# A ninth slot of weights, one late weight instead of two: a Hymba layer (RG-LRU beside window attention) on one Trainium2 core

## The chip, the cores and the metric

The kernel runs on one core of a Trainium2 chip. The metric is device time in microseconds (us) of one execution; the time of a version is the median of its runs. PE is the matrix engine, DVE the vector engine, ACT the activation engine, POOL the general engine, SP the engine that issues the transfers; PEclk is the clock that PE was granted, as a share of 2.4 GHz (its other level is 1.2 GHz).

## The reference, cut to what matters

One layer on a prompt of 4096 positions (width 1024) and 8 sample positions, in fp32:

```python
xn = rms_norm(x, g_pre)
proj = xn @ w_in     # rnn 512 | rnn gate 512 | q 512 | k 128 | v 128 | attention gate 512
# recurrent group: width-4 causal conv, then
#   h_t = a_t*h_{t-1} + sqrt(1-a_t^2)*(i_t*x_t),  a_t = sigmoid(L)^(8 r_t)
# attention group: window of 128, 8 q heads, 2 kv heads, bucketed bias, a sink per head
y = x + rms_norm(concat(h * silu(gate_r), o * silu(gate_a)) @ w_out, g_post)
```

The sample positions attend to a cache of 128 rows, and the states and windows are outputs too.

## The kernel before, in words

Every fp32 operand of a product is split into a high and a low part, and `mm3` (L122, L123, L124) makes one product of three matmuls. The prompt is cut into 11 chunks (ten of 384 columns, and the first of 256 with the 8 sample columns). Three stages follow each other.

**The recurrent stage** goes over the chunks. `load_A` loads row tiles `xs` (L153; four slots), ACT squares them (L161, `sq`), POOL scales them, `prep_A` transposes them on PE (L176, `pt`) into `xh`/`xl`, which are also stored for the second stage. `proj_A` makes the products `pr` with eight weights, four for the recurrent input and four for its gate; ACT copies a product out (`xr` L298, `xc` L302). `rnn_A` makes the gates (`gt`), with ACT's `thr`, `thi` (L333, L334). `scan_A` takes one square root over four tiles (L348, `uu`, ahead of which ACT loads another function table), scans (L352), multiplies (L361) and stores `hh` to `mix_d` (L362).

**The attention stage** goes over the chunks again: keys `pk`, values `pv`, four queries `pq` and four gates `pga` from ten weights, then for each block of 128 the scores `S` (L601, L602), a softmax (`tt`), its transpose `pT` (L635) and the output `po` (L644). For chunk 0 the order is V, Q0, K, Q1, Q2, Q3, G0, G1, G2, G3, and weight numbers run V=13, Q=8 to 11, K=12, G=14 to 17. **The output stage** (L819 to L821) multiplies by `w_out`, whose tiles of `mix_d` come through staging tiles `xf`.

A weight is loaded by `load_w`: a transfer of 512 KB into one of two staging slots `ws` (L105), a copy on ACT (`wh`, L111) and a subtraction on DVE (`wl`, L112). `wh` and `wl` are slots of the pool `wpool`. It has eight, which the recurrent stage's eight weights fill; a weight of the attention stage gets one when the last product with an old weight is done. Eight of the ten weights fit. The last two, G2 and G3, lie in the pool `pbl`, which is opened over the recurrent stage's late buffers (`uu`, `xc`, `sg`, `thr`, `thi`, `tt`, `aa`, `hh`), so these two can only be written when that stage's last buffers are free.

The order of the instructions isn't written by hand. A scheduler puts each engine's list in an order of its own, by a model of the machine, and each engine then runs its list strictly in that order. A change of the pools therefore changes the lists of all five engines. Names in the lists carry chunk and column tile: `gt_10_2` is the gate of chunk 10, tile 2; a number behind that tells buffers apart.

Of the kernel before, what the change touches and what calls it, by code (L numbers as in the profile page):

```python
# [9 lines left out]
F32 = mybir.dt.float32  # L10
# [5 lines left out]
P = 128  # L16
D = 1024
KD = D // P
DR = 512
HD = 64  # L20
NH = 8
# [3 lines left out]
NSAMP = 8  # L25
SEQ = 4096
STEP = 384
# [17 lines left out]
def hymba_kernel(ctx: ExitStack, tc: tile.TileContext, ins, outs):  # L45
# [15 lines left out]
    act = nc.scalar.activation  # L61

    const = ctx.enter_context(tc.tile_pool(name="const", bufs=1))
    wpool = ctx.enter_context(tc.tile_pool(name="wpool", bufs=8))
    xpool = ctx.enter_context(tc.tile_pool(name="xpool", bufs=12))
    stage = ctx.enter_context(tc.tile_pool(name="stage", bufs=2))
    dram = ctx.enter_context(tc.tile_pool(name="dram", bufs=1, space=bass.MemoryType.DRAM))
# [15 lines left out]
    def ps_t(n):  # L83
        if phase[0] == "A":
            return ps[2].tile([P, 512], F32, tag="t", name=n, bufs=2)
        return ps[1].tile([P, 512], F32, tag="t", name=n, bufs=1)

    def ps_v(n):
        if phase[0] == "A":
            return ps_t(n)  # L90
        return ps[1].tile([P, 512], F32, tag="v", name=n, bufs=1)
# [11 lines left out]
    def load_w(src, n, pool, bufs=None, spare=None, eng=nc.vector, fast=False):  # L103
        ws = (spare or stage).tile([P, KD, P], F32, tag="ws", name=f"ws_{n}")
        nc.sync.dma_start(ws, src)  # L105
        wh = pool.tile([P, KD, P], F32R, tag="wh", name=f"wh_{n}", bufs=bufs)
        wl = pool.tile([P, KD, P], F32R, tag="wl", name=f"wl_{n}", bufs=bufs)
        if fast:
            nc.vector.tensor_copy(wh, ws)
        else:  # L110
            act(wh, ws, AF.Copy)  # L111
        eng.tensor_sub(wl, ws, wh)  # L112
        return wh, wl

    def load_w_in(m, pool=None, bufs=None, spare=None, eng=nc.vector, fast=False):
        return load_w(w_in_v[:, :, m * P:(m + 1) * P], f"in{m}", pool or wpool, bufs, spare, eng, fast)
# [101 lines left out]
        return p1, p2  # L218


    grow = stage.tile([KD, P], F32, tag="xf", name="grow", bufs=4)
    nc.sync.dma_start(grow, norm_pre.rearrange("o (k p) -> (o k) p", p=P))
    cp0 = ps_t("cp0")
    nc.tensor.transpose(cp0[:, 0:KD], grow, ident[:KD, :KD])
# [5 lines left out]
    xA = ([], [])  # L230
    prep_A(0, xn, range(KD), xA)

    crow = stage.tile([32, P], F32, tag="xf", name="crow", bufs=4)
    nc.sync.dma_start(crow[0:16, :], conv_w.rearrange("o t (c p) -> (o t c) p", p=P))
    nc.sync.dma_start(crow[16:20, :], conv_b.rearrange("o (c p) -> (o c) p", p=P))
    nc.sync.dma_start(crow[20:24, :], b_ga.rearrange("o (c p) -> (o c) p", p=P))
# [133 lines left out]
    ksT = const.tile([P, NSAMP], F32, name="ksT")  # L370
    vsT = const.tile([P, NSAMP], F32, name="vsT")
# [44 lines left out]
    wB = {}  # L416
# [24 lines left out]
    for ci in range(NCH):  # L441
        for item in A_ORDER:
            f, s = item[0], st[ci]
            c = int(item[1:] or 0)
# [55 lines left out]
    def prep_B(ci, src, on_act, half=()):  # L500
        t0, npt, ns = chunks[ci]
        W = npt + ns
        xh, xl = [], []
        for k in range(KD):
            xf = stage.tile([P, STEP], F32, tag="xf", name=f"xf_{src.name}_{k}", bufs=4)
            nc.sync.dma_start(xf[:, :W], src[:, k, :])
            h, l = split_x(xf[:, :W], W, f"{src.name}_{k}", on_act, k in half)
            xh.append(h)
            xl.append(l)
        return xh, xl  # L510
# [169 lines left out]
        return {"K": key, "V": value, "Q": query, "G": gate, "U": unit, "M": scale}  # L680

    def attend_sample(pool):
        def window(new, cache, dst, n):
            pr = ps_t(f"pr_{n}")
            nc.tensor.transpose(pr[:NSAMP, 0:P], new, ident)
            row = pbl.tile([NSAMP, P], F32, tag="sh", name=f"row_{n}", bufs=2)
            nc.vector.tensor_copy(row, pr[:NSAMP, 0:P])
            win = pbl.tile([P, NSAMP, P], F32, tag="wh", name=f"win_{n}", bufs=2)
            rows = cache[0].rearrange("b j v d -> j b (v d)")
            nc.sync.dma_start(win[0:112], rows[1:113])  # L690
            nc.sync.dma_start(win[112:P - 1], rows[113:P])
            nc.sync.dma_start(win[P - 1:P], row)
            nc.sync.dma_start(dst[0].rearrange("b j v d -> j b (v d)"), win)
            return win

        kw = window(ksT, ck, o_ks, "k")
        vw = window(vsT, cv, o_vs, "v")
        yield
        kT = pbl.tile([P, NSAMP, P], F32, tag="wl", name="kT_s", bufs=2)
        for half in range(2):  # L700
            pt = ps_t(f"ptk_{half}")
            for b in range(4):
                nc.tensor.transpose(pt[:, b * P:(b + 1) * P], kw[:, half * 4 + b, :], ident)
            nc.vector.tensor_copy(kT[:, half * 4:half * 4 + 4].rearrange("p b k -> p (b k)"), pt)
        yield
        T = pbl.tile([P, NSAMP, P], F32, tag="wl", name="T_s", bufs=2)[:NH]
        for half, f in enumerate((ps_t, ps_v)):
            S = f(f"S_samp{half}")[:NH].rearrange("p (b k) -> p b k", k=P)
            for b in range(4):
                nc.tensor.matmul(S[:, b, :], qz[:, half * 4 + b, :], kT[:, half * 4 + b, :], start=True, stop=True)  # L710
            nc.vector.tensor_tensor(T[:, half * 4:half * 4 + 4], S,
                                    bs.rearrange("p (o k) -> p o k", o=1).broadcast_to([NH, 4, P]), op=ALU.add)
        m = pool.tile([NH, 4, NSAMP], F32, name="m_s")
        nc.vector.tensor_reduce(m[:, 0], T, axis=mybir.AxisListType.X, op=ALU.max)
        nc.vector.tensor_scalar(m[:, 1], m[:, 0], sk8, None, op0=ALU.max)
        nc.vector.tensor_sub(T, T, m[:, 1].rearrange("p (b o) -> p b o", o=1).broadcast_to([NH, NSAMP, P]))
        act(T, T, AF.Exp)
        nc.vector.tensor_reduce(m[:, 2], T, axis=mybir.AxisListType.X, op=ALU.add)
        act(m[:, 3], m[:, 1], AF.Exp, scale=-1.0, bias=sk8)
        nc.vector.tensor_add(m[:, 2], m[:, 2], m[:, 3])  # L720
        nc.vector.reciprocal(m[:, 0], m[:, 2])
        nc.vector.tensor_mul(T, T, m[:, 0].rearrange("p (b o) -> p b o", o=1).broadcast_to([NH, NSAMP, P]))
        yield
        pt = ps_t("pt_s")
        for b in range(NSAMP):
            nc.tensor.transpose(pt[:, b * NH:(b + 1) * NH], T[:, b, :], ident[:NH, :NH])
        PT = pool.tile([P, NSAMP, NH], F32, name="PT_s")
        nc.vector.tensor_copy(PT.rearrange("p b h -> p (b h)"), pt[:, 0:NSAMP * NH])
        yield
        po = ps_v("po_s")  # L730
        for b in range(NSAMP):
            nc.tensor.matmul(po[:, b * NH:(b + 1) * NH], vw[:, b, :], PT[:, b, :], start=True, stop=True)
        pov = po[:, 0:NSAMP * NH].rearrange("p (b c two) -> p two c b", c=4, two=2)
        at = pool.tile([P, 4, NSAMP], F32, name="at_s")
        for par in range(2):
            for kv in range(2):
                act(at[par * HD:(par + 1) * HD, 2 * kv:2 * kv + 2, :],
                    pov[kv * HD:(kv + 1) * HD, par, 2 * kv:2 * kv + 2, :], AF.Copy)
        nc.vector.scalar_tensor_tensor(at, at, 0.5, sgS, op0=ALU.mult, op1=ALU.mult)
        n = chunks[0][1]  # L740
        nc.sync.dma_start(mix_d[0][:, 4:8, n:n + NSAMP], at)
# [7 lines left out]
    pbl, pb, pb1 = [c.__enter__() for c in cms]  # L749
    xB = load_x(0)  # L750
    for item in B_FIRST:
        if item[0] in "KVQG":
            m = {"K": 12, "V": 13, "Q": 8, "G": 14}[item[0]] + (int(item[1]) if item[0] in "QG" else 0)
            wB[m] = load_w_in(m) if len(wB) < 8 else load_w_in(m, pbl, 2)
    state = [{} for _ in chunks]
    state[0]["xs"] = xB
    work = [chunk_B(ci, state[ci], state[ci - 1]) for ci in range(NCH)]
    for ci in range(NCH):
        for item in B_ORDER if ci else B_FIRST:
            f, args = item[0], [int(i) for i in item[1:]]  # L760
# [10 lines left out]

    wC = [load_w_out(e) for e in range(8)]
    sample = attend_sample(pb)
    turn = 0

    order = [*range(1, NCH), 0]
    for ci in order:
# [14 lines left out]
        for j, (xsrc, ydst, rows, off) in enumerate(tiles):  # L792
            n = f"{ci}_{j}"
# [3 lines left out]
            if final:  # L797
                cuts = [(0, 512), (512, 768), (768, D)]
                po = [f(f"out_{n}_{i}") for i, f in enumerate((ps_mm, ps_t, ps_v))]
            else:  # L800
                cuts = [(0, 512), (512, D)]
                if turn % 3 == 0:
                    po = [ps_mm(f"out_{n}_{i}") for i in range(2)]
                else:
                    po = ps_s(f"out_{n}")
                    po = [po[:, 0:512], po[:, 512:D]]
                turn += 1
            po = [p[:, 0:c[1] - c[0]] for p, c in zip(po, cuts)]
# [27 lines left out]
            for i, (p, c) in enumerate(zip(po, cuts)):  # L836
                sq = stage.tile([P, 512], mybir.dt.bfloat16, tag="sqc", name=f"sqc_{n}_{i}", bufs=1)
                act(sq[:rows, :c[1] - c[0]], p[:rows], AF.Square, scale=1.0 / 32.0, accum_out=ss[:rows, i:i + 1])  # L838
                if final and i:
                    po[i] = stage.tile([P, STEP], F32, tag="xf", name=f"pg_{i}", bufs=4)[:, 0:c[1] - c[0]]  # L840
                nc.vector.tensor_mul(po[i][:rows], p[:rows], gpost[:rows, c[0]:c[1]])  # L841
            nc.vector.tensor_scalar(ss[:rows, 0:1], ss[:rows, 0:1], ss[:rows, 1:2], EPS, op0=ALU.add, op1=ALU.add)  # L842
            if final:
# [58 lines left out]
```

## Time and profile before

| | |
|---|---|
| median of 3 runs | 1448.07 us (1445.95 to 1451.45) |
| the profiled execution | 1450.88 us |
| its span | 1449.2 us |
| PE, PEld busy | 97%, 91% of the span |
| DVE, ACT, POOL busy | 63%, 55%, 30% |
| mean granted PE clock | 0.991 |

The profile is of one execution. Busy time of PE is time in which a matmul runs; a matmul at the lower clock counts as busy too, so a slow stretch is seen in PEclk and in the number of matmuls of a stretch. A bracket at the end of a row of the timeline is the idle time of the engine ahead of that instruction, and what ended it.

### The profile page before, as it was taken

To read this page: it belongs to the slowest core of one execution; us is meant where nothing else is said; L and a number is where in the kernel's file an instruction comes from. 1 tells how busy PE (TensorE), PEld (TensorE's weight loads), DVE (VectorE), ACT (ScalarE), POOL (GpSimd) and SP (SyncE) were. 2 spreads that over 40 slices of the span, in tenths; PEclk is the share of its full clock that TensorE was granted. 3 is DMA by queue.
4 is the path that set the end of the run, shared out by engine and by line. 5 is a ranking of instruction groups with operands and counts; after the bars stand their busy time and mean duration, and the time that the engine had idled before them with its cause. 6 is when DMAs were issued, how large, how long until landed. Compare 5 with 4: busy or idle time off the path is not lost.

```text
span 1449.2 us, 24120 instructions
## 1 busy us (share of the span) xinstructions
PE 1403.5 (97%) x8127; PEld 1323.5 (91%) x8127; DVE 914.3 (63%) x2258; ACT 800.0 (55%) x2055; POOL 440.9 (30%) x876
## 2 busy tenths in 40 slices
PE   5999999999999889999999999999999999999998
PEld 4999989999999779999999999999998888888886
DVE  6778877777777767557566566566784445334433
ACT  4566656665555656577676676576783222222211
POOL 3233332222421033354463453453543000000000
PEclk9999999999999999999999999999999999999999
DMA  9324453434236330330320320330444534433431
GB/s 274 133 83 157 149 168 138 153 131 139 97 121 196 90 117 22 119 106 12 110 99 12 110 99 12 109 99 12 162 133 146 167 134 142 145 133 133 147 129 60
DMA packets 115029, 170.23 MB, mean 117 GB/s; under 512 B 12215, under 2 KB 98823, under 8 KB 114907
## 3 DMA queue, kind: packets, MB, share of 16 engines
q1 hardware_dynamic: 114906, 168.71, 34.7%
q8 instruction: 64, 1.05, 0.3%
q14 instruction: 59, 0.48, 0.1%
HBM read 100.19 MB, written 68.50 MB: 116 GB/s over the span
## 4 chain that ended last, share of the span: by engine, by line
PE 68%; DVE 3%; ACT 2%; DMA 1%; issue 1%; SPq 0%; POOL 0%; POOLq 0%; DVEq 0%; ACTq 0%
PE out L819 8%; PE out L821 8%; PE out L820 8%; PE pga L122 4%; PE pga L123 4%; PE pga L124 4%; PE pq L123 4%; PE pq L122 4%; PE pq L124 4%; PE po L661 3%; PE S L601 2%; PE S L602 2%; PE pT L635 2%; PE pr L122 1%; PE pr L124 1%; PE pr L123 1%
## 5 line engine op out<-in xcount | busy, mean ns | idle before, releaser
L123 PE MATMUL pr<-xl,wh_in 128*128 128x384 f32 (+1 forms) x688 | 231.8, 338 | 0.0
L122 PE MATMUL pr<-xh,wh_in 128*128 128x384 f32 (+1 forms) x688 | 220.1, 340 | 10.8 <-ACT xc L302 10.8
L124 PE MATMUL pr<-xh,wl_in 128*128 128x384 f32 (+1 forms) x688 | 230.0, 336 | 0.0
L819 PE MATMUL out<-wh_out,xh_mix_d 128*128 128x512 f32 (+1 forms) x520 | 201.3, 387 | 0.0
L820 PE MATMUL out<-wl_out,xh_mix_d 128*128 128x512 f32 (+1 forms) x520 | 200.9, 386 | 0.0
L821 PE MATMUL out<-wh_out,xl_mix_d 128*128 128x512 f32 (+1 forms) x520 | 200.5, 386 | 0.0
L838 ACT ACTIVATE sqc<-out 128x512 bf16<-128x512 f32 (+2 forms) x67 | 39.2, 585 | 192.5 <-PE out L821 182.4
L122 PEld LDWEIGHTS pr<-xh,wh_in 128*128 128x128 f32 x688 | 129.9, 191 | 12.5 <-ACT xc L302 12.2
L627 ACT ACTIVATE tt<-tt,nm 128x129 f32<-128x129 f32 x256 | 100.0, 393 | 72.0 <-DVE nm L624 71.8
L841 DVE TENSOR_TENSOR out<-out,gpost 128x512 f32<-128x512 f32 (+1 forms) x65 | 45.4, 699 | 147.6 <-ACT sqc L838 147.0
L123 PEld LDWEIGHTS pr<-xl,wh_in 128*128 128x128 f32 x688 | 131.3, 191 | 0.7 <-issue 0.7
L124 PEld LDWEIGHTS pr<-xh,wl_in 128*128 128x128 f32 x688 | 131.1, 191 | 0.0
L122 PE MATMUL pq<-xh_B,wh_in 128*128 128x384 f32 (+1 forms) x352 | 117.7, 335 | 1.8 <-ACT qz L571 1.1
L123 PE MATMUL pga<-xl_B,wh_in 128*128 128x384 f32 (+1 forms) x352 | 118.8, 337 | 0.0
L122 PE MATMUL pga<-xh_B,wh_in 128*128 128x384 f32 (+1 forms) x352 | 117.7, 334 | 0.7 <-ACT qz L571 0.7
L123 PE MATMUL pq<-xl_B,wh_in 128*128 128x384 f32 (+1 forms) x352 | 118.0, 335 | 0.0
L124 PE MATMUL pq<-xh_B,wl_in 128*128 128x384 f32 (+1 forms) x352 | 117.8, 335 | 0.0
L124 PE MATMUL pga<-xh_B,wl_in 128*128 128x384 f32 (+1 forms) x352 | 117.2, 333 | 0.0
L141 POOL TENSOR_TENSOR rs_c<-ssc,mhalf 128x1 f32<-128x1 f32 (+1 forms) x33 | 20.5, 622 | 315.0 <-DVE ssc L842 276.1
L819 PEld LDWEIGHTS out<-wh_out,xh_mix_d 128*128 128x128 f32 x520 | 97.7, 188 | 19.9 <-issue 0.2
L821 PEld LDWEIGHTS out<-wh_out,xl_mix_d 128*128 128x128 f32 x520 | 97.7, 188 | 19.7
L820 PEld LDWEIGHTS out<-wl_out,xh_mix_d 128*128 128x128 f32 x520 | 97.7, 188 | 19.3
(258 smaller groups left out, 3563.8 us busy)
## 6 DMA issues: line engine op xcount, KB each, us to landing
xs<-in_x_prompt_dram SPq DMA_DIRECT2D x32, 512.0 KB
xr<-in_x_prompt_dram SPq DMA_DIRECT2D x32, 512.0 KB
out_dram<-xr SPq DMA_DIRECT2D x31, 512.0 KB
xT_d<-xh SPq DMA_DIRECT2D x80, 192.0 KB
xT_d<-xl SPq DMA_DIRECT2D x80, 192.0 KB
xf_mix_d<-mix_d SPq DMA_DIRECT2D x80, 192.0 KB
xh_B<-xT_d SPq DMA_DIRECT2D x80, 192.0 KB
xl_B<-xT_d SPq DMA_DIRECT2D x80, 192.0 KB
```

Of the source, the lines that this page charges most:

```text
L122: nc.tensor.matmul(out, wh, xh, start=first, stop=False)
L123: nc.tensor.matmul(out, wh, xl, start=False, stop=False)
L124: nc.tensor.matmul(out, wl, xh, start=False, stop=last)
L601: nc.tensor.matmul(o, qa, kt[:, kv, 0, kr], start=True, stop=False)
L602: nc.tensor.matmul(o, qa, kt[:, kv, 1, kr], start=False, stop=True)
L627: act(tt[:, g, 0:P + 1], tt[:, g, 0:P + 1], AF.Exp, scale=-1.0, bias=nm[:, g:g + 1], accum_out=sm[:, g:g + 1])
L661: nc.tensor.matmul(pog[:, :, r], v.rearrange("p l d -> p (l d)"), w[:, :, r], start=i == 0, stop=i == 2)
L819: nc.tensor.matmul(p, a, wh, start=st, stop=False)
L820: nc.tensor.matmul(p, a, wl, start=False, stop=False)
L821: nc.tensor.matmul(p, b, wh, start=False, stop=sp)
L838: act(sq[:rows, :c[1] - c[0]], p[:rows], AF.Square, scale=1.0 / 32.0, accum_out=ss[:rows, i:i + 1])
L841: nc.vector.tensor_mul(po[i][:rows], p[:rows], gpost[:rows, c[0]:c[1]])
```

## The change

Nine slots in `wpool` instead of eight; three staging tiles `xf` instead of four; only G3 lies in `pbl` (one slot of each kind there). The sample's attention used the two slots of `pbl` for its windows and transposed keys; now it has one there and takes a slot of `wpool` for the other.

```diff
-    wpool = ctx.enter_context(tc.tile_pool(name="wpool", bufs=8))
+    wpool = ctx.enter_context(tc.tile_pool(name="wpool", bufs=9))
...
-            xf = stage.tile([P, STEP], F32, tag="xf", name=f"xf_{src.name}_{k}", bufs=4)
+            xf = stage.tile([P, STEP], F32, tag="xf", name=f"xf_{src.name}_{k}", bufs=3)
...
-        def window(new, cache, dst, n):
+        def window(new, cache, dst, n, home):
...
-            win = pbl.tile([P, NSAMP, P], F32, tag="wh", name=f"win_{n}", bufs=2)
+            win = home.tile([P, NSAMP, P], F32, tag="wh", name=f"win_{n}", bufs=1 if home is pbl else None)
...
-        kw = window(ksT, ck, o_ks, "k")
-        vw = window(vsT, cv, o_vs, "v")
+        kw = window(ksT, ck, o_ks, "k", pbl)
+        vw = window(vsT, cv, o_vs, "v", wpool)
         yield
-        kT = pbl.tile([P, NSAMP, P], F32, tag="wl", name="kT_s", bufs=2)
+        kT = pbl.tile([P, NSAMP, P], F32, tag="wl", name="kT_s", bufs=1)
...
-        T = pbl.tile([P, NSAMP, P], F32, tag="wl", name="T_s", bufs=2)[:NH]
+        T = wpool.tile([P, NSAMP, P], F32, tag="wl", name="T_s")[:NH]
...
-            wB[m] = load_w_in(m) if len(wB) < 8 else load_w_in(m, pbl, 2)
+            wB[m] = load_w_in(m) if len(wB) < 9 else load_w_in(m, pbl, 1)
```

(The tiles `grow`, `crow` and `pg`, which share the slots of `xf`, have 3 in place of 4 too.) `pbl` is 8 KB smaller, so the pools opened behind it lie lower: the six tiles `vs` of the attention stage now lie over the recurrent stage's four `hh`, which they didn't before.

The lists move in three places that matter below. **First**, ACT in the recurrent stage, where the square root of chunk 5 is taken. `sq_7_1` is the square of a row tile that has just been loaded, `xr_6_1` and `xc_6_1` free the product that PE wants to write next. Before:

```order
L179 ACTIVATE xh_6_7_3289<-pt_6_7_3285,gpre_148 128x384
L348 ACT_TABLE_LOAD
L348 ACTIVATE uu_5_3042<-uu_5_3042 128x1536
L161 ACTIVATE sq_7_1_3374,ss_7_1_3373<-xs_7_1_3371 128x1024
L298 ACTIVATE xr_6_1_3345<-pr_6_1_1_3295 128x384
L302 ACTIVATE xc_6_1_3350<-pr_6_1_1_3295,cT_250 128x384
```

The change:

```order
L338 ACTIVATE thr_5_3_3234<-thr_5_3_3234,sp4n_257 128x384
L161 ACTIVATE sq_7_1_3374,ss_7_1_3373<-xs_7_1_3371 128x1024
L348 ACT_TABLE_LOAD
L348 ACTIVATE uu_5_3042<-uu_5_3042 128x1536
L161 ACTIVATE sq_7_2_3383,ss_7_2_3382<-xs_7_2_3380 128x1024
L298 ACTIVATE xr_6_1_3345<-pr_6_1_1_3295 128x384
L302 ACTIVATE xc_6_1_3350<-pr_6_1_1_3295,cT_250 128x384
```

One square moved ahead of the table load and the square root, and a second one ahead of `xr`. The same happens at the square root of chunk 6. The square roots of chunks 3, 4, 7 and 8 had this order before and keep it.

**Second**, the end of the recurrent stage, on ACT and PE: the gates of chunk 10. ACT before:

```order
L333 ACTIVATE thr_10_1_5428<-gt_10_1_5421,hba_252 128x384
L334 ACTIVATE thi_10_1_5429<-gt_10_1_5421,hbx_253 128x384
L337 ACTIVATE tt_10_1_5432<-thr_10_1_5428,sp2_256 128x384
L111 ACTIVATE wh_in14_5687<-ws_in14_5685 128x1024
L338 ACTIVATE thr_10_1_5428<-thr_10_1_5428,sp4n_257 128x384
L302 ACTIVATE xc_10_3_5514<-pr_10_3_1_5459,cT_250 128x384
L564 ACTIVATE sq_0_0_5771<-pq_0_0_5746 64x256
L565 ACTIVATE sq_0_0_5771<-pq_0_0_5746 64x256
L111 ACTIVATE wh_in15_5693<-ws_in15_5691 128x1024
L333 ACTIVATE thr_10_0_5447<-gt_10_0_5440,hba_252 128x384
L334 ACTIVATE thi_10_0_5448<-gt_10_0_5440,hbx_253 128x384
```

ACT in the change:

```order
L316 ACTIVATE thg_10_3_5522<-pr_10_3_2_5460 128x384
L111 ACTIVATE wh_in15_5693<-ws_in15_5691 128x1024
L333 ACTIVATE thr_10_1_5428<-gt_10_1_5421,hba_252 128x384
L334 ACTIVATE thi_10_1_5429<-gt_10_1_5421,hbx_253 128x384
L337 ACTIVATE tt_10_1_5432<-thr_10_1_5428,sp2_256 128x384
L338 ACTIVATE thr_10_1_5428<-thr_10_1_5428,sp4n_257 128x384
L302 ACTIVATE xc_10_3_5514<-pr_10_3_1_5459,cT_250 128x384
L111 ACTIVATE wh_in16_5699<-ws_in16_5697 128x1024
L333 ACTIVATE thr_10_0_5447<-gt_10_0_5440,hba_252 128x384
L334 ACTIVATE thi_10_0_5448<-gt_10_0_5440,hbx_253 128x384
```

Ahead of `thr_10_1` now stands the copy of weight 15, where that of weight 11 stood, and ahead of `thr_10_0` that of weight 16, where that of weight 15 stood. On PE the gate `gt_10_2` stood between products of the attention stage:

```order
L123 MATMUL pk_0_5779<-xl_B0_7_5647,wh_in12_5663 128x264
L124 MATMUL pk_0_5779<-xh_B0_7_5645,wl_in12_5664 128x264
L122 MATMUL gt_10_2_5526<-xk_10_2_5413,gwh_291 128x384
L123 MATMUL gt_10_2_5526<-xk_10_2_5413,gwh_291 128x384
L124 MATMUL gt_10_2_5526<-xk_10_2_5413,gwl_292 128x384
L122 MATMUL gt_10_2_5526<-xk_10_2_5413,gwh_291 128x384
L123 MATMUL gt_10_2_5526<-xk_10_2_5413,gwh_291 128x384
L124 MATMUL gt_10_2_5526<-xk_10_2_5413,gwl_292 128x384
L122 MATMUL pq_0_1_5813<-xh_B0_0_5617,wh_in9_5669 128x264
```

In the change:

```order
L124 MATMUL gt_10_2_5526<-xk_10_2_5413,gwl_292 128x384
L122 MATMUL gt_10_3_5545<-xk_10_3_5519,gwh_291 128x384
L123 MATMUL gt_10_3_5545<-xk_10_3_5519,gwh_291 128x384
L124 MATMUL gt_10_3_5545<-xk_10_3_5519,gwl_292 128x384
L122 MATMUL gt_10_3_5545<-xk_10_3_5519,gwh_291 128x384
L123 MATMUL gt_10_3_5545<-xk_10_3_5519,gwh_291 128x384
L124 MATMUL gt_10_3_5545<-xk_10_3_5519,gwl_292 128x384
L549 MATMUL pvt_0_5737<-ident_101,vt_0_5734 128x128 x2
L122 MATMUL pk_0_5779<-xh_B0_0_5617,wh_in12_5663 128x264
```

The three gates `gt_10_0`, `gt_10_2`, `gt_10_3` now follow each other, and the products `pk` and `pq_0_1`, which stood between them, come behind.

**Third**, the last scan of the recurrent stage, on DVE (`sq_0_1` frees a product of PE for `pq_0_2`). Before, the queries stood ahead of it, and the copies of weights 16 and 17 far behind; in the change:

```order
L352 SCALAR_TENSOR_TENSOR hh_10_3_5587<-aa_10_3_5557,hl_9_3_5195,thi_10_3_5553 128x384
L361 TENSOR_TENSOR hh_10_0_5566<-hh_10_0_5566,sg_10_0_5351 128x384
L361 TENSOR_TENSOR hh_10_1_5573<-hh_10_1_5573,sg_10_1_5284 128x384
L361 TENSOR_TENSOR hh_10_2_5580<-hh_10_2_5580,sg_10_2_5418 128x384
L566 TENSOR_TENSOR sq_0_1_5838<-pq_0_1_5813,sq_0_1_5838 64x256
L567 TENSOR_TENSOR sq_0_1_5838<-pq_0_1_5813,sq_0_1_5838 64x256
L361 TENSOR_TENSOR hh_10_3_5587<-hh_10_3_5587,sg_10_3_5524 128x384
L112 TENSOR_TENSOR wl_in17_5706<-ws_in17_5703,wh_in17_5705 128x1024
```

and ACT in the change:

```order
L348 ACT_TABLE_LOAD
L348 ACTIVATE uu_10_5420<-uu_10_5420 128x1536
L564 ACTIVATE sq_0_1_5838<-pq_0_1_5813 64x256
L565 ACTIVATE sq_0_1_5838<-pq_0_1_5813 64x256
L571 ACTIVATE qz_282<-pq_0_1_5813 64x8 x2
L111 ACTIVATE wh_in17_5705<-ws_in17_5703 128x1024
L553 ACTIVATE vs_0_0_5740<-pvt_0_5737 128x2x64
L484 ACTIVATE kt_0_5778<-pk_0_5779 64x256 x2
```

So weight 17 now comes shortly behind the square root and ahead of `vs` and `kt`, which the first scores need; before, `kt` and `vs_0_0` stood ahead of the square root. Besides these, weight 13 (V) is converted as early as chunk 4 of the recurrent stage, into the ninth slot; before, it came at the end of chunk 9.

## Rows read from the trace of the kernel before

**Rows 1.** Page, busy time by engine (share of the span, instructions)

```profile
PE 1403.5 (97%) x8127; PEld 1323.5 (91%) x8127; DVE 914.3 (63%) x2258; ACT 800.0 (55%) x2055; POOL 440.9 (30%) x876
```

**Rows 2.** Stretches: length, busy (instructions) of PE, PEld, DVE, ACT, POOL; PEclk, DMA, GB/s

```profile
360.00:380.00 20.00, 17.72 (x95) 17.33 (x95) 15.41 (x30) 12.52 (x20) 11.68 (x15) 0.91 0.33 123
...
460.00:480.00 20.00, 18.39 (x126) 18.19 (x124) 14.72 (x26) 9.79 (x16) 1.26 (x2) 1.00 0.89 274
480.00:500.00 20.00, 16.55 (x105) 16.03 (x106) 15.79 (x39) 14.94 (x32) 0.44 (x3) 0.83 0.18 53
500.00:520.00 20.00, 11.79 (x78) 10.20 (x77) 18.04 (x58) 11.87 (x39) 2.74 (x6) 0.88 0.12 41
...
1200.00:1220.00 20.00, 20.00 (x97) 16.13 (x96) 13.57 (x23) 7.23 (x18) 1.35 (x2) 1.00 0.45 147
```

**Rows 3.** Waits of PE over the span: us in total, times, longest

```profile
PE pr L122 <- ACT xc L302: 10.8, 6, 2.3
...
PE po L644 <- ACT ph L639: 3.5, 1, 3.5
...
PE pT L635 <- DVE tt L632: 2.2, 1, 2.2
```

**Rows 4.** Timeline of PE: start, us, instruction [idle before]

```profile
199.41 0.45 PE L122 MATMUL pr<-xh,wh_in 128*128 128x384 f32 x1 [1.51 <-ACT xc L302]
...
242.78 0.45 PE L122 MATMUL pr<-xh,wh_in 128*128 128x384 f32 x1 [0.71 <-ACT xc L302]
...
366.94 0.44 PE L122 MATMUL pr<-xh,wh_in 128*128 128x384 f32 x1 [2.28 <-ACT xc L302]
...
410.79 0.45 PE L122 MATMUL pr<-xh,wh_in 128*128 128x384 f32 x1 [1.74 <-ACT xc L302]
```

**Rows 5.** Timeline of ACT at the square root of chunk 7

```profile
360.96 1.06 ACT L161 ACTIVATE sq<-xs 128x1024 bf16<-128x1024 f32 x1 [2.22 <-DMA xs<-in_x_prompt_dram]
...
366.23 0.66 ACT L302 ACTIVATE xc<-pr,cT 128x384 f32<-128x384 f32 x1
```

**Rows 6.** Timeline of ACT, first square behind the root of chunk 5

```profile
279.71 1.06 ACT L161 ACTIVATE sq<-xs 128x1024 bf16<-128x1024 f32 x1 [0.68 <-DMA xs<-in_x_prompt_dram]
```

**Rows 7.** Timeline, loads of weights: issue on SP

```profile
462.30 0.38 SPq L105 DMA_DIRECT2D ws_in<-in_w_in_dram  x1
...
469.97 0.38 SPq L105 DMA_DIRECT2D ws_in<-in_w_in_dram  x1
```

**Rows 8.** Timeline of ACT, copies of weights that waited for these loads

```profile
466.64 1.06 ACT L111 ACTIVATE wh_in<-ws_in 128x1024 fp32r<-128x1024 f32 x1 [4.31 <-DMA ws_in<-in_w_in_dram]
...
476.44 1.06 ACT L111 ACTIVATE wh_in<-ws_in 128x1024 fp32r<-128x1024 f32 x1 [1.51 <-DMA ws_in<-in_w_in_dram]
```

**Rows 9.** Timeline of PE, gates of tiles 0 and 2 of chunk 10

```profile
475.62 0.28 PE L124 MATMUL pk<-xh_B,wl_in 128*128 128x264 f32 x1
475.74 0.34 PE L122 MATMUL gt<-xk,gwh 128*128 128x384 f32 x1
...
481.63 0.69 PE L122 MATMUL gt<-xk,gwh 128*128 128x384 f32 x1 [3.23 <-ACT thi L334]
482.11 0.52 PE L123 MATMUL gt<-xk,gwh 128*128 128x384 f32 x1
```

**Rows 10.** Timeline of ACT, the last square root and the two late weights

```profile
497.14 1.49 ACT L348 ACTIVATE uu<-uu 128x1536 f32<-128x1536 f32 x1
...
513.65 2.00 ACT L111 ACTIVATE wh_in<-ws_in 128x1024 fp32r<-128x1024 f32 x2 [3.69 <-DMA mix_d<-hh]
```

**Rows 11.** Timeline of DVE, the last scan

```profile
500.25 1.96 DVE L350 TENSOR_TENSOR thi<-thi,uu 128x384 f32<-128x384 f32 x4
...
505.32 2.84 DVE L352 TENSOR_TENSOR_SCAN hh<-aa,hl,thi 128x384 f32<-128x384 f32 x3
...
510.04 1.49 DVE L361 TENSOR_TENSOR hh<-hh,sg 128x384 f32<-128x384 f32 x3
```

**Rows 12.** Timeline of PE, the first scores of chunk 0

```profile
493.95 0.48 PE L601 MATMUL S<-kt,sq 128*128 128x128 f32 x2
```

More of the change, by code (lines that the diff above doesn't have):

```diff
@@ L218, in project2 @@
         return p1, p2
-    grow = stage.tile([KD, P], F32, tag="xf", name="grow", bufs=4)
+    grow = stage.tile([KD, P], F32, tag="xf", name="grow", bufs=3)
     nc.sync.dma_start(grow, norm_pre.rearrange("o (k p) -> (o k) p", p=P))
@@ L231, in hymba_kernel @@
     prep_A(0, xn, range(KD), xA)
-    crow = stage.tile([32, P], F32, tag="xf", name="crow", bufs=4)
+    crow = stage.tile([32, P], F32, tag="xf", name="crow", bufs=3)
     nc.sync.dma_start(crow[0:16, :], conv_w.rearrange("o t (c p) -> (o t c) p", p=P))
@@ L839, in hymba_kernel @@
                 if final and i:
-                    po[i] = stage.tile([P, STEP], F32, tag="xf", name=f"pg_{i}", bufs=4)[:, 0:c[1] - c[0]]
+                    po[i] = stage.tile([P, STEP], F32, tag="xf", name=f"pg_{i}", bufs=3)[:, 0:c[1] - c[0]]
                 nc.vector.tensor_mul(po[i][:rows], p[:rows], gpost[:rows, c[0]:c[1]])
```

## The prediction

> **What bounds the kernel now.** I read the page first: PE is busy 97% of the span [rows 1], so whatever the change does, it does by the few per cent in which PE waits or runs at the lower clock. The table of stretches then tells where these lie. The output stage has none: 20.00 of 20 us busy at full clock [rows 2]. The recurrent stage has isolated ones, as between 360 and 380 us, where PE was busy 17.72 us and the granted clock fell to 0.91. The passage from the recurrent to the attention stage has most: between 460 and 520 us PE was busy 18.39, 16.55 and 11.79 us, so it idled 13.3 of 60 us, and the granted clock was 0.83 and 0.88 in the last two stretches. The waits of PE name the causes [rows 3]: a product `pr` that waits for ACT's `xc`, 10.8 us in six times, all in the recurrent stage; and single waits of 3.5 us for `ph` and 2.2 us for `tt` in the passage. The timeline shows the 3.5 us at its source: the copies of the two late weights sat in ACT's list ahead of `ph`, and ACT idled 3.69 us until the stores of `hh` had landed [rows 10]. This is the wait that the change shortens, as one of the two copies no longer lies over those buffers.
>
> **The clock** matters beside the waits. Behind the idle time of 3.23 us ahead of a gate, a matmul of 384 columns took 0.52 us, against 0.34 us in the gate before it [rows 9]: 1.2 GHz after 2.4. In the stretch with the 2.28 us wait, the missing 0.09 of the clock, over 20 us, is about 1.8 us [rows 2, 4]; that went the same way.
>
> **Part 1, the recurrent stage.** Removed or added work: none but the early conversion of weight 13. That puts one ACT copy of 1.06 us [rows 8] and one subtraction on DVE into chunk 4, and takes them out of the end of chunk 9. I cost it at 0: it is hidden by PE, which has products queued there; if that cover were gone it would cost about 1 us.
>
> What costs is the order at the square root. Where the square comes first, ACT stands still until its row tile has landed, 2.22 us in the row shown, and only then loads its table, takes the root, squares a second tile and frees PE's product: 5.3 us from 360.96 to `xc` at 366.23 [rows 5]. Where the root comes first, it runs in the time in which the tile travels, and the square then waits only 0.68 us [rows 6]; PE doesn't wait at all. The four chunks with the square first cost PE 1.51, 0.71, 2.28 and 1.74 us [rows 4], 6.24 us in all, a mean of 1.56. The change gives two more chunks this order: 2 × 1.56 = 3.1 us. One of the four took the clock with it, for 1.8 us; two more at that rate are 0.9. **Term: +4 us.** The low end is two waits like the shortest, +1.4; the high end two like the longest with the clock, 2 × (2.28 + 1.8) = +8.2. I take the mean, since PE's other work in those chunks is of the same length. A gain isn't excluded, as the lists around chunks 4, 7 and 8 are slightly reordered too; I allow 2 us for it, the two shortest of the four waits (0.71 + 1.51).
>
> **Part 2, the passage.** Here the idle times of 13.3 us are exchanged for others.
>
> Gone: the wait of 3.5 us for `ph` behind two late weights and the 2.2 us for `tt`, most likely, since scan and stores are now through before the first softmax.
>
> New, first: the three last gates follow each other on PE, and ahead of two of them ACT must copy a weight. A load took 4.3 us (462.30 to 466.64) to 6.5 us (469.97 to 476.44) from issue to the copy's start [rows 7, 8], the long one while 274 GB/s moved [rows 2]. With weight 13 out of the way, one load fewer is ahead of the others, but each still needs its staging slot, which comes free with the copy two weights before. Before, `gt_10_0` ran at 475.74, behind 12 products of `pk` at 0.12 us each [rows 9] that now come later, so PE is ready for it at 474.3. Weight 15 takes the place of weight 14, whose copy began at 476.44, and is some 2 us sooner for the load that is gone: 474.6. With the copy and `thr`, `thi`, PE goes on at 476: 1.7 us. Copies followed each other by 4.9 us on the mean (466.64 to 476.44, two steps [rows 8]), so weight 16 comes at 479.5, and `gt_10_2`, for which PE is ready at 477.1, starts at about 480.8: 3.7 us. `gt_10_3` waits for the gates of `gt_10_2` and its own operand, 1.9 us, and `pvt_0` for `vt`, now behind the gates on ACT, 1.5 us. Together 8.8 us, against 3.2 us for this gate before [rows 9].
>
> New, second: the last scan. `gt_10_3` ends at about 487, and ACT's work up to the root takes some 5 us, so the root comes at about 492 instead of 497.14 [rows 10], and the recurrent stage ends earlier. But DVE's list has the query `sq_0_1` behind the scan. Four products in 1.96 us, four scans of 0.95 and three multiplications of 0.5 [rows 11] are 7.3 us; behind a root of 1.49 us and with its own two subtractions `sq_0_1` is done at about 502, and `pq_0_2` on PE, which needs its product's space, stands from about 496: 5.5 to 8 us, I take 6.5. Before, that work lay beside scores and queries.
>
> New, third: `wh_in17` still waits for the stores of `hh`, and `kt` for it in ACT's list. Before, the copy began 2.1 us behind the last multiplication (511.53 to 513.65) [rows 10, 11]; so the first scores, at 493.95 before [rows 12], come at 507 to 509. PE has `pq_0_2` in the meantime. About 3 us of waiting for scores and for `ksT` remain.
>
> The sum of the new waits is 8.8 + 6.5 + 3 = 18.3 us, against 13.3. The clock's share is much the same, since each passage has one long wait early and one late. **Term: +5 us.** Its low end is 0: weights that land as fast as the fastest, 4.3 us, take some 3 us from the gates, and the scan's wait may be the 5.5. The high end is +9: the scan's wait at 8, and scores that come 2 to 3 us later.
>
> By the Trainium skill (DMA: Bandwidth & Descriptors, section "Anatomy of one DMA — SWDGE (gpsimd) path") a transfer takes about 2.0 us plus its bytes over 436 GB/s, an estimate of 3.2 us for 512 KB; by it the weights would land 1 to 3 us sooner and the passage would cost about +2 instead of +5. The rows of 4.3 and 6.5 us speak against it here.
>
> **Part 3, the rest.** Three staging tiles instead of four for the output stage: PE is busy 20.00 of 20 us there [rows 2] with products of a whole chunk while the next chunk's tiles are loaded and split; 0, and if that cover were gone, a tile would show as a wait of some 2 us, as the stores of `hh` did. The sample's attention has the same instructions in other slots: 0.
>
> **Sum:** 4 + 5 = +9 us. The profiled execution took 1450.88 us, 2.8 above the median, so this would be 1460 for it and 1457 for the median of 1448.07. A measurement of this kernel can tell about 0.5%, or 7.2 us, from no change.
>
> **Rivals.**
> 1. *Faster, by 7 to 12 us: about 1438.* The ninth slot does what a slot is for. The recurrent stage ends 5 us earlier, `ph` (3.5) and `tt` (2.2) no longer wait, and with them goes the slow stretch at 0.88 of the clock. The point that decides is `pq_0_2`: if its product's space is free at 496, or other products cover it, the 6.5 us and the 3 us behind them fall away. That leaves 8.8 us of waits against 13.3, and with no late wait the missing 0.12 of the clock between 500 and 520 us, 2.4 us, goes too: −7 with the recurrent stage at 0. Weights as fast as the fastest (3 us) and that stage at −2 make it −12. For it: those waits are the largest in the rows. Against it: DVE's list, which puts `sq_0_1` behind three multiplications. By the Trainium skill (Perfetto Trace Analysis, "Optimization Strategy") repeated gaps on the engine that should be saturated can mean too few buffers for the next tile; by that rule this rival would win. The gaps shown above are single ones, though, each with another name.
> 2. *No change, −4 to +4: 1448.* The waits of the recurrent stage trade places without changing their sum, and the passage moves its 13 to 18 us about. For it: PE's work is the same, and waits of this size go and come wherever the lists move. Against it: both terms above have the same sign.
> 3. *Slower, by 16 to 22 us: about 1467.* Each new wait is followed by matmuls at 1.2 GHz: two in the recurrent stage (8.2) and, in the passage, 8 us of waiting for the scan with some 4 us of slow matmuls behind it. For it: 0.83 and 0.88 of the clock in this passage before [rows 2].
> 4. *The change doesn't free what it means to*: G3's weight still waits for `hh`, and `vs` now lies over `hh`, so the attention stage's first values wait for the same stores. That is inside my forecast (third new wait); alone it would be worth about +3.
>
> **Chances.** Forecast (+3 to +16) 0.54; rival 1 0.11; rival 2, with rival 4 alone, 0.24; rival 3 0.11. The forecast's lower part, about 0.18, lies within 0.5%. So faster 0.11, same 0.42, slower 0.47. The range leaves out rival 1 and the top: 1444 (rival 2's low end) to 1466 (between the forecast's high ends, 8.2 + 9 = +17, and rival 3).
>
> **What would show it.** In the changed profile: waits of `pr` for `xc` in the recurrent stage that sum to about 4 us more, with two new ones near 280 and 322 us; between 470 and 490 us waits ahead of `gt_10_0`, `gt_10_2` and `gt_10_3`; a wait of 5 to 8 us ahead of `pq_0_2` near 500 us, ended by DVE's `sq` (L567); no wait for `ph` of over 1 us; the output stage at 20.00 of 20. I am wrong if the `pr` waits stay near 10.8 us, or if `pq_0_2` starts at once.

## The result, and the profile after

The change is slower: 1456.8 us (median of 6 runs, 1452.98 to 1460.78) against 1447.56 us before in the same session (6 runs, 1445.95 to 1451.45). The ratio is 1.0071, with a 95% interval of 1.0054 to 1.0088, or 10 us (8 to 13). The profiled execution took 1460.78 us, with a span of 1459.1 us, so it is the slowest of the six; against the one of before its span is 9.9 us longer.

The waits of PE, over the span of the change [rows 3 before]; a row names who waited, for what, the sum in us, the number of times and the longest:

```profile
PE pr L122 <- ACT xc L302: 15.1, 8, 2.7
...
PE pq L122 <- ACT qz L571: 6.0, 1, 6.0
PE gt L122 <- ACT thi L334: 5.8, 3, 2.8
...
PE pq L122 <- DVE ksT L531: 2.0, 1, 2.0
...
PE pvt L549 <- ACT vt L544: 1.4, 1, 1.4
PE gt L123 <- DVE xk L313: 1.1, 1, 1.1
PE S L602 <- DVE kt L486: 0.8, 1, 0.8
```

The waits for `ph` and `tt` (3.5 and 2.2 us [rows 3]) are gone. The waits of `pr` rose from 10.8 us in six to 15.1 us in eight. In the passage the waits come to 17.5 us (with 0.4 us for `sq`), where they were 13.2; a wait for `kl` near the end of the attention stage (0.7 and 1.0 us) is left out of both.

The stretches of the change, with the columns of [rows 2]:

```profile
360.00:380.00 20.00, 18.10 (x98) 17.79 (x97) 14.80 (x28) 13.38 (x22) 10.28 (x13) 0.91 0.45 156
400.00:420.00 20.00, 18.12 (x99) 17.78 (x99) 12.46 (x23) 13.34 (x21) 6.83 (x9) 0.91 0.32 112
...
480.00:500.00 20.00, 11.98 (x53) 10.24 (x54) 13.36 (x27) 15.52 (x26) 0.00 (x0) 0.66 0.30 90
500.00:520.00 20.00, 11.31 (x71) 10.70 (x70) 15.70 (x43) 9.41 (x28) 4.30 (x7) 0.78 0.11 41
```

The granted clock was 0.66 and 0.78 between 480 and 520 us, where it was 0.83 and 0.88 [rows 2]; in these 40 us 124 matmuls ran, where 183 had run.

How much of it arose where? The same instruction of SP's queue tells. The stores of chunk 9's last three `hh`, which end the recurrent stage's steady part, and the store of the last values `vr`, near the end of the attention stage, were issued before at 458.70 and 1063.56:

```profile
458.70 1.79 SPq L362 DMA_DIRECT2D mix_d<-hh  x3
...
1063.56 0.34 SPq L559 DMA_DIRECT2D out_dram<-vr  x1
```

and in the change 4.9 and 9.65 us later:

```profile
463.58 1.79 SPq L362 DMA_DIRECT2D mix_d<-hh  x3
...
1073.21 0.34 SPq L559 DMA_DIRECT2D out_dram<-vr  x1
```

So the recurrent stage lost 4.9 us, the passage with the rest of the attention stage 4.8, and what follows nothing that can be told. These are differences of single executions, and such times scatter: in two versions below whose roots and squares stand as in the change (all tiles put back, and only `kt` put back), the stores of chunk 9 were issued at 465.32 and at 459.95.

In the recurrent stage, the new waits stand at the square roots of chunks 5 and 6. PE in the change:

```profile
286.05 0.44 PE L122 MATMUL pr<-xh,wh_in 128*128 128x384 f32 x1 [1.78 <-ACT xc L302]
...
327.91 0.44 PE L122 MATMUL pr<-xh,wh_in 128*128 128x384 f32 x1 [1.29 <-ACT xc L302]
```

and ACT ahead of the first of them:

```profile
280.07 1.06 ACT L161 ACTIVATE sq<-xs 128x1024 bf16<-128x1024 f32 x1 [2.02 <-DMA xs<-in_x_prompt_dram]
...
282.53 1.49 ACT L348 ACTIVATE uu<-uu 128x1536 f32<-128x1536 f32 x1
...
285.33 0.66 ACT L302 ACTIVATE xc<-pr,cT 128x384 f32<-128x384 f32 x1
```

This is the pattern of [rows 5]: ACT stands 2.02 us for the row tile with the root and `xc` queued behind, where before the square waited 0.68 us behind the root [rows 6].

In the passage PE of the change waits for the gates, then for the query behind the scan:

```profile
481.54 0.44 PE L122 MATMUL gt<-xk,gwh 128*128 128x384 f32 x1 [1.89 <-ACT thi L334]
...
485.67 0.69 PE L122 MATMUL gt<-xk,gwh 128*128 128x384 f32 x1 [2.80 <-ACT thi L334]
...
507.94 0.59 PE L122 MATMUL pq<-xh_B,wh_in 128*128 128x264 f32 x1 [5.96 <-ACT qz L571]
```

The last row's cause lies one step further back, on DVE: ACT's `qz` at 507.51 waited for DVE's `sq`, which stands behind the scan. ACT, then DVE:

```profile
507.51 0.37 ACT L571 ACTIVATE qz<-pq 64x8 f32<-64x8 f32 x2 [4.73 <-DVE sq L567]
...
501.46 3.74 DVE L352 TENSOR_TENSOR_SCAN hh<-aa,hl,thi 128x384 f32<-128x384 f32 x4
505.12 1.47 DVE L361 TENSOR_TENSOR hh<-hh,sg 128x384 f32<-128x384 f32 x3
506.62 0.42 DVE L566 TENSOR_TENSOR sq<-pq,sq 64x256 fp32r<-64x256 f32 x1
507.05 0.43 DVE L567 TENSOR_TENSOR sq<-pq,sq 64x256 fp32r<-64x256 f32 x1
```

### The profile page after: what moved, and what is told of

It is laid out like the page before. It is cut to its first block, busy times and chain, and to the rows that moved or that the text cites. A ratio compares the mean times of both kernels' runs of the same rounds, so it can differ in the third digit from the quotient of the medians.

```text
span 1459.1 us, 24138 instructions
## 1 busy us (share of the span) xinstructions
PE 1405.8 (96%) x8127; PEld 1325.8 (91%) x8127; DVE 914.2 (63%) x2258; ACT 800.0 (55%) x2055; POOL 442.6 (30%) x876
## 4 chain that ended last, share of the span: by engine, by line
PE 89%; DMA 3%; ACT 3%; DVE 2%; issue 1%; SPq 1%; POOL 0%; POOLq 0%; DVEq 0%; ACTq 0%
PE out L819 8%; PE out L821 8%; PE out L820 8%; PE pr L122 7%; PE pr L123 7%; PE pr L124 7%; PE pga L122 4%; PE pga L123 4%; PE pga L124 4%; PE pq L122 4%; PE pq L123 4%; PE pq L124 4%; PE po L661 3%; DMA xs<-in_x_prompt_dram 2%; PE S L601 2%; PE pT L635 2%
## 5 line engine op out<-in xcount | busy, mean ns | idle before, releaser
L122 PE MATMUL pr<-xh,wh_in 128*128 128x384 f32 (+1 forms) x688 | 221.0, 340 | 15.1 <-ACT xc L302 15.1
L122 PEld LDWEIGHTS pr<-xh,wh_in 128*128 128x128 f32 x688 | 130.0, 191 | 17.5 <-ACT xc L302 17.1
```

The costliest lines, as they stand in the source:

```text
L122: nc.tensor.matmul(out, wh, xh, start=first, stop=False)
```

## Experiments

The result leaves one question: nine slots were to help, and the lists moved against them, but what moved the lists? My theory after the result is that two separate things did: the early copy of weight 13 in the recurrent stage, and, in the passage, the tiles that came to lie over other buffers as `pbl` shrank. The rivals are that the ninth slot itself costs (its loads and copies ahead of the gates), that the waits of `pr` only trade places, and that the output stage has a share. All ratios are to the kernel before on the same chip, with 95% intervals; on it 0.001 is 1.4 us. The edits are cut to what matters and written out; in the kernels some stand on one line. Where an edit says `issue_after`, it only queues an instruction behind another of the same engine and adds no wait for its end.

**The place of the tiles alone.**

```diff
+    pbl.tile([P, 2048], F32, name="pad")
```

> The change with an empty tile of 8 KB in pbl, so that vs, kt and all behind them lie where they lay before over the recurrent stage's buffers; nine slots stay. In its lists the queries stand ahead of the last scan again and pk between the last gates. Theory (the passage costs because of the order, and the order comes from which buffers lie under vs and kt): about 5 us less than the change, 1450 to 1453 us; the wait of 6.0 us ahead of pq_0_2 gone, gates waiting 3 to 5 us instead of 7. Rival (the passage costs because of the nine slots: the weights' loads and copies ahead of the gates): 1455 to 1458 us, and the waits ahead of gt_10_0 and gt_10_2 stay at 4.7 us in all.

Measured: 1451.8 us, ratio 1.0034 (1.0017 to 1.0051), as the theory said; the gates wait even less than the 3 to 5 us expected, and a wait of 4.5 us for `sgb` came that the theory didn't name. The first lines of its waits from 440 us on:

```profile
PE pga L122 <- DVE sgb L582: 4.5, 1, 4.5
PE S L601 <- DVE sq L566: 2.4, 2, 1.8
PE gt L122 <- ACT thi L334: 1.8, 2, 1.1
```

The wait ahead of `pq_0_2` is gone, and the gates wait 1.8 instead of 5.8 us, although the copies of weights 15 and 16 still stand ahead of `thr_10_1` and `thr_10_0` in ACT's list. So the nine slots don't cost in the passage: the place of the tiles does. SP's queue says the same of this version:

```profile
465.32 1.79 SPq L362 DMA_DIRECT2D mix_d<-hh  x3
...
1065.04 0.34 SPq L559 DMA_DIRECT2D out_dram<-vr  x1
```

The two stores lie 599.7 us apart, against 609.6 in the change and 604.9 before. With the places put back, this one execution of nine slots was 5 us shorter here than the one of eight. The medians don't bear out a gain: the 0.0034 that is left is what the recurrent stage costs by the test of weight 13 below (0.0033), which leaves nothing for the passage.

**Root first, in the change and in the kernel before.** Both have the same edit, in `load_A` and `scan_A`:

```diff
-                act(sq[:rows], xs[:rows], AF.Square, scale=1.0 / 32.0, accum_out=ss[:rows])
+                with tc.issue_after(rootA[ci - 2]) if ci > 1 and j else nullcontext():
+                    act(sq[:rows], xs[:rows], AF.Square, scale=1.0 / 32.0, accum_out=ss[:rows])
...
-        act(uu[:, :, :W], uu[:, :, :W], AF.Sqrt, scale=-0.25)
+        rootA[ci] = act(uu[:, :, :W], uu[:, :, :W], AF.Sqrt, scale=-0.25).ins
```

> The change with every square of a row tile (tiles 1 and 2 of a chunk) queued on ACT behind the square root of two chunks before. Theory (the waits of pr for xc cost the recurrent stage): the waits between 40 and 440 us fall from 12.6 us to about 3 (chunk 0 alone), with two dips of the clock of 1.8 us gone: 10 to 13 us less than the change, 1444 to 1447 us. Rival (those waits only trade places with later ones): 1454 to 1458 us.

> The kernel before with the same rule of root first; eight slots, nothing else. Theory: the four waits of 6.2 us and one dip of the clock (1.8 us) go: about 8 us less than before, 1438 to 1442 us. Rival (the waits trade places): 1446 to 1449 us.

Measured: 1447.6 us, ratio 1.0004 (0.9989 to 1.0019), for the change; 1437.57 us, ratio 0.9948 (0.9929 to 0.9967), for the kernel before. The change gained 0.0067, 9.7 us, just short of the 10 to 13 expected; the kernel before gained 7.5, as expected. The waits of `pr` between 40 and 440 us, in the kernel before with root first:

```profile
PE pr L122 <- ACT xc L302: 2.1, 1, 2.1
PE pt L176 <- POOL xs L166: 1.1, 2, 0.8
```

They didn't trade places: of 8.6 us in this stretch one wait, chunk 0's, is left. In the change 1.7 us are left of 12.6, but here PE waits 4.4 us for the row tiles that POOL scales, as the squares now come late:

```profile
PE pt L176 <- POOL xs L166: 4.4, 5, 0.9
PE pr L122 <- ACT xc L302: 1.7, 1, 1.7
```

The clock came back with them: the stretch from 360 to 380 us was granted 1.00 in both, where it was 0.91.

**Both together.**

```diff
+    pbl.tile([P, 2048], F32, name="pad")
...
+                with tc.issue_after(rootA[ci - 2]) if ci > 1 and j else nullcontext():
```

> The change with both: the empty tile of 8 KB and root first. Theory: both terms go and the late weights no longer hold ph as long; the two gains add up, 5 + 11 = 16 us less than the change, 1438 to 1443 us, at or a little under the kernel before with root first. Rival: less than 5 us under the change.

Measured: 1439.76 us, ratio 0.9957 (0.9940 to 0.9973). Against the change's 1.0071 this is 16 us less: the two effects add up. It is not under the kernel before with root first (0.9948).

**Three staging tiles alone**, in the kernel before:

```diff
-            xf = stage.tile([P, STEP], F32, tag="xf", name=f"xf_{src.name}_{k}", bufs=4)
+            xf = stage.tile([P, STEP], F32, tag="xf", name=f"xf_{src.name}_{k}", bufs=3)
...
```

(The same for `grow`, `crow` and `pg`.)

> The kernel before with three staging tiles xf instead of four, nothing else. Theory (their cover holds): within 2 us of before, and the output stage at 20.00 of 20 us. Rival (part of the loss comes from the output stage or the move between stages): 3 us or more above before.

Measured: 1445.19 us, ratio 0.9998 (0.9986 to 1.0009). The cover holds:

```profile
1200.00:1220.00 20.00, 20.00 (x97) 16.13 (x96) 13.72 (x23) 6.06 (x13) 1.02 (x2) 1.00 0.54 182
```

**Weight 13 copied late**, in the change:

```diff
-            wB[m] = load_w_in(m) if len(wB) < 9 else load_w_in(m, pbl, 1)
+            with tc.issue_after(rootA[9]) if m == 13 else nullcontext():
+                wB[m] = load_w_in(m) if len(wB) < 9 else load_w_in(m, pbl, 1)
```

> The change, with ACT's copy of weight 13 queued behind the square root of chunk 9, where it stood before; the roots of chunks 5 and 6 then stand ahead of the squares again, while the passage keeps the change's order (gates in a row, queries behind the scan). Theory (the early copy of weight 13 is what turned the recurrent stage's lists): the waits of pr for xc fall back from 12.6 to about 8.6 us, 1450 to 1453 us, 4 to 5 above before. Rival (other parts of the change turned them): 1456 to 1458 us.

Measured: 1452.61 us, ratio 1.0038 (1.0024 to 1.0052). From 40 to 440 us, and then from 440 us on:

```profile
PE pr L122 <- ACT xc L302: 7.4, 5, 2.1
...
PE pq L122 <- ACT qz L571: 4.9, 1, 4.9
PE gt L122 <- ACT thi L334: 3.2, 2, 1.6
```

The recurrent stage is as before again, with five waits instead of seven, while the passage keeps its wait behind the scan. So the early copy turned the lists of the recurrent stage. Not the 1.06 us of the copy cost 4.8 us (0.0033), but the order that it set off.

**Only `kt` and what lies behind it put back**, in the change:

```diff
-            kt = pb.tile([P, 2, 2, P + STEP], F32R, tag="kt", name=f"kt_{ci}", bufs=2)
+            kt = (ci or pb.tile([P, 2048], F32, name="pad")) and pb.tile([P, 2, 2, P + STEP], F32R, tag="kt", name=f"kt_{ci}", bufs=2)
```

> The change with the empty tile of 8 KB between vs and kt: vs still lies over hh, kt and all behind it lie as before. In its lists pk stands between the gates again, but kt, vs and the first scores still behind the scan's stores and weight 17. Theory (two separate costs: kt over the gates' weights puts the gates in a row, vs over hh puts the scores behind the scan): the gates' waits fall from 7 to about 2 us, the scores still come late, at 505 us or later, and the sum lies between the change and the version with all tiles as before: 1452 to 1456 us. Rival (vs over hh costs nothing, only kt): 1450 to 1452 us, as that version.

Measured: 1453.19 us, ratio 1.0053 (1.0033 to 1.0073), in the range of the theory, but its interval meets both that of the change and that of all tiles put back. The gates wait as little as with all tiles put back (1.7 us, against 5.8 in the change), and the first scores come late, at 507.05 us:

```profile
496.94 0.59 PE L122 MATMUL pq<-xh_B,wh_in 128*128 128x264 f32 x1 [2.90 <-ACT qz L571]
507.05 0.79 PE L601 MATMUL S<-kt,sq 128*128 128x128 f32 x2 [4.47 <-ACT kt L484]
```

The passage's waits sum to 11.0 us, against 10.9 with all tiles put back (0.7 us at the stage's end left out in both). So `kt` and the tiles behind it are what put the gates in a row. What `vs` over `hh` costs beside this stays open: the medians differ by 0.0019, 2.7 us, within their intervals. The trace hints at the clock, as the sums of the waits are equal, but this isn't shown: between 480 and 520 us it was granted 0.82 and 0.75 here, and 0.91 and 0.99 with all tiles put back.

**Nine slots with the lists in order**: the empty tile, root first, weight 13 late, and the load of weight 17 traced only at the item G3 of chunk 0.

```diff
-        if item[0] in "KVQG":
+        if item[0] in "KVQG" and item != "G3":
...
+            if ci == 0 and item == "G3":
+                wB[17] = load_w_in(17, pbl, 1)
```

> The change with the empty tile of 8 KB in pbl, root first, the copy of weight 13 behind the root of chunk 9, and weight 17's load traced only ahead of its own product, in chunk 0. Theory (the nine slots are worth something once the lists don't cost): no wait of po for ph over 1 us, 1 to 5 us under the kernel before with root first: 1432 to 1437 us. Rival (nothing is left to gain by a slot): 1436 to 1440 us, as that kernel.

Measured: 1439.96 us, ratio 0.9957 (0.9941 to 0.9974). The wait for `ph` was gone, and the time wasn't under the kernel before with root first: the rival.

**Eight slots against nine, with the late weights' copies behind `ph`.** In the eight-slot kernel (before with root first) weights 16 and 17, in the nine-slot one (the last, with weight 17):

```diff
-            act(phs, pt, AF.Copy)
+            keep[n] = act(phs, pt, AF.Copy).ins
...
+            if ci == 0 and item == "G0":
+                with tc.issue_after(keep["0_0_0"]):
+                    wB.update({m: load_w_in(m, pbl, 2) for m in (16, 17)})
```

> Eight slots: the kernel before with root first, and the copies of the two late weights (16, 17) queued on ACT behind ph of the first block. Theory (ph waited only for these copies in ACT's list): the wait of po for ph, 6.7 us in the kernel before with root first, falls under 1.5 us, the products of weight 16 wait 1 to 3 us for it instead: 3 to 5 us under that kernel, 1432 to 1435 us, 0.990 to 0.993 of before. Rival (the wait moves whole to the products of weight 16): 1436 to 1439 us, 0.994 to 0.996.

> Nine slots, arranged alike: the change with the empty tile of 8 KB in pbl, root first, the copy of weight 13 behind the root of chunk 9, and the copy of the one late weight (17) queued behind ph of the first block. Theory (a slot is worth only the wait for the late weights, which the order can hide as well): within 3 us of the version with eight slots in the same call. Rival (the ninth slot is worth something of its own, as only one weight is late): 4 us or more under it.

Measured: 1437.91 us, ratio 0.9952 (0.9935 to 0.9968), with eight; 1436.89 us, ratio 0.9945 (0.9931 to 0.9958), with nine. For eight the theory fell: the wait of `po` for `ph` went from 6.7 us, in the kernel before with root first, to 4.9 us and not under 1.5. ACT in the kernel before with root first:

```profile
497.66 2.00 ACT L111 ACTIVATE wh_in<-ws_in 128x1024 fp32r<-128x1024 f32 x2 [2.60 <-DMA mix_d<-hh]
```

and with the copies behind `ph`:

```profile
499.74 0.31 ACT L606 ACTIVATE vx<-vs 64x128 fp32r<-64x128 f32 x1 [2.60 <-DMA mix_d<-hh]
...
504.01 0.60 ACT L639 ACTIVATE ph<-pT 128x512 fp32r<-128x512 f32 x1
504.63 2.00 ACT L111 ACTIVATE wh_in<-ws_in 128x1024 fp32r<-128x1024 f32 x2
```

The 2.60 us for the stores of `hh` passed from the copies to the next in ACT's list, `vx`, a tile that lies in `pbl` as the late weights do; a dozen of its copies stand ahead of `ph`. So moving the weights took 1.8 us off the wait, about their own 2.0 us of copying, and the wait for the stores stayed. Between eight and nine lies 1 us, as the theory for nine said: in these two versions a ninth slot is worth nothing that can be told. They aren't alike in all else. The eight-slot one keeps the 4.9 us for `ph`; the nine-slot one has no such wait and others in its place (10.1 and 11.0 us in all from 440 us on). The nine-slot version is, with the eight-slot one with root first, the fastest found, some 8 us under the kernel before.

## Why the prediction was right

The time forecast was 1457, and 1456.8 came. That they agree to 0.2 us is luck, as the interval of the loss is 8 to 13 us; that the forecast lies inside that interval is not luck alone, as both terms came near their size: +4 for the recurrent stage (4.9 by SP's queue, 4.8 by weight 13 copied late, 1.0071 against 1.0038), +5 for the passage (4.8 by the queue, 5.4 by the tiles put back, 1.0071 against 1.0034), 0 for the rest (−0.3, 0.9998). The two figures from ratios are uncertain by about 3 us each.

- **The order at the root** held. The two new waits measured 1.78 and 1.29 us against a mean of 1.56 taken. The sum took the other chunks to stay as they were, and that wasn't so in one: the wait in chunk 4 grew from 0.71 to 1.51 us. With that the waits from 40 to 440 us went from 8.6 to 12.6 us, +4.0 where +3.1 was forecast. The clock took a further dip, in the stretch from 400 to 420 us (1.00 before, 0.91 after), not behind one of the two new waits but behind one that had been there (1.74, now 1.88 us). So the clock's 0.9 us was priced for the wrong waits, and that a dip came at all is in part luck: in the trace with only `kt` put back, whose roots and squares stand as in the change, the stretch from 320 to 340 us was granted 0.91 and that from 360 to 380 us 1.00.
- **The gates in a row** held: 1.89, 2.80 and 1.14 us for `thi`, 1.11 for `xk` and 1.42 for `vt` are 8.4 us, against the 8.8 of the walk. Their reason was put too narrowly. The copies of weights ahead of `thr` make PE wait only since no product of `pk` lies between the gates; with the tiles put back the copies stand there still, and the gates wait 1.8 us.
- **The query behind the scan** held: 5.96 us, against 6.5.
- **Scores and `ksT`**: 2.8 us, against 3.
- "The clock's share is much the same" failed for the granted clock, 0.66 and 0.78 where 0.83 and 0.88 had been, and held for the time. The waits grew by 4.3 us and the passage by 4.8, which leaves slower matmuls an estimated 0.5 us. The way of counting that the prediction used in the recurrent stage, missing clock times 20 us, would give 5 us more here; it counts the clock of idle time too, and fewer matmuls ran at it.
- **The loads of weights.** In the change, the load issued at 474.14 was there for the copy at 479.49, 5.35 us, and others took 3.75 us. By the Trainium skill (DMA: Bandwidth & Descriptors, "Anatomy of one DMA — SWDGE (gpsimd) path") the estimate was 3.2 us. The section gives its fit for DMAs on GpSimd's path, and these loads are issued by SP, so the rows decide and don't contradict it: from issue to landing, 18 loads of weights took 4.7 us at the median in the change, and 32 loads `xr` of the same 512 KB 3.2 us.
- **The rivals.** Rival 1, faster, would have needed queries that don't wait for the scan; with the tiles put back they don't, and even then the change is 0.0034 slower, from the recurrent stage. Rival 3 was right in that the clock took a share, and wrong in its size. By the Trainium skill (Perfetto Trace Analysis, "Optimization Strategy") repeated gaps can mean too few buffers. That didn't carry the rival here: the waits that repeat, of `pr`, went with the order (one is left with root first), and with the lists in order nine slots and eight are 1 us apart.

What the forecast lacked is why the lists moved. It read the moved lists and priced them. That, by their addresses, `kt` now lay over the gates' weights, where nothing of it can be written before the last gate, didn't enter as a cause; `vs` over `hh` stood only in rival 4.

## What to carry to other kernels

Where a scheduler orders the instructions, a slot more is three edits: the slot, a copy that can now go early, and a shift of every pool opened behind it. Look which earlier buffers each later tile comes to lie over, and try the slot with the old places (an empty tile is enough) before judging it. And look for an instruction that waits for a transfer at the head of a queue, with the release of the bottleneck engine's space behind it: queueing it behind the root was worth some 7.5 us in the kernel before (0.9948; 5 to 10 us), more than the slot.

## What the runs showed of the hardware

A wait's own length doesn't tell what it costs. In the recurrent stage of the change, PE waited 1.78 us at 286 us and the stretch from 280 to 300 us was granted 1.00 of the clock; the wait of 1.88 us ahead of 414.45 us came with 0.91 and 99 matmuls in its stretch, where the 1.74 us of before [rows 4] had come with 1.00 and 110. The change, then the kernel before:

```profile
280.00:300.00 20.00, 18.22 (x108) 17.92 (x107) 16.11 (x30) 12.53 (x20) 11.93 (x15) 1.00 0.38 140
...
414.45 0.45 PE L122 MATMUL pr<-xh,wh_in 128*128 128x384 f32 x1 [1.88 <-ACT xc L302]
```

```profile
400.00:420.00 20.00, 18.26 (x110) 17.93 (x109) 14.37 (x27) 13.46 (x23) 8.04 (x11) 1.00 0.37 123
```

So the one cost no more than its length, the other by estimate 1.7 us more: 11 matmuls fewer, at some 0.17 us each, less the 0.14 us by which the wait is longer. In the trace with only `kt` put back, two waits of one length differed so: 1.78 us near 282 us came with 1.00 in its stretch, 1.77 us near 324 us with 0.91.
